# A Hyena mixer's Fourier transforms as plain float32 matmuls, with the convolution in order and wider sums with i

## The chip, the cores and the metric

The kernel runs on one core of one Trainium2 chip. The metric is the device time of one execution in microseconds; the time given for a kernel is the median of several executions.

## The reference: what is computed

One block of a diffusion transformer on a sequence of 1024 positions with 1024 channels, in float32. After a modulated RMS norm, one wide projection gives the inputs of two mixers, differential attention and Hyena; their gated sum goes through an output projection, and a SwiGLU follows. The change touches only the Hyena part:

```python
def hyena_branch(u, ...):                       # u: 1024 positions x 1536 channels
    u = short_conv(u, conv_w, conv_b)           # three taps along the positions
    parts = split(u, 3)                         # 512 channels each
    hk = hyena_filters(...)                     # spectra of 2 filters, made by a small MLP
    z = parts[0]
    for n in range(2):
        z = parts[n + 1] * fftconv(z, hk[:, n], dbias[n])
    return z

def fftconv(u, hk, dbias):                      # a circular convolution of length 2048
    return irfft(rfft(u, n=2048) * hk, n=2048)[:1024] + u * dbias
```

## The kernel before, in words

Channels lie on the 128 partitions, positions along the free axis. The kernel is written for a scheduling layer: the program is recorded in the order of its lines, each instruction with its dependences, and at build time a list scheduler puts the instructions of each engine in order, by the order of recording as the priority and by estimated durations. On the chip every engine works through its own list strictly in that order. So a later part's instruction can stand ahead of an earlier part's where the scheduler saw the engine free; the projections fill TensorE's gaps in this way.

The stages that matter:

1. **Start and filters** (`ORDER`, L26, names the order of recording). `load_mf` (M) loads the transform's matrix; `ada_rows`, `x_stats`, `x_scale` and `modulate` make the normed input `h_hi`, `h_lo`. For four filter blocks (2 filters x 2 groups of 256 channels), `filter_begin`, `filter_mid`, `filter_mid2` and `filter_end` make eight pieces of the filter each (`make`, L378), transform them with TensorE (`spec`, L397, matmuls at L408), combine two results into a sum and a difference (`sd_from_psum`, L255) and finish with butterflies on DVE (`dft8_even`, `dft8_odd`). The spectrum goes to DRAM (`kspec`).
2. **Hyena** (L521 to L671). `raw_tile` (L495) projects one tile of 128 output channels: `wload` loads weights and splits them (`whi` on ACT at L132, `wlo` on DVE), then 2 x 24 matmuls at L140 follow. There are 12 such tiles for Hyena (`praw`) and 16 for the gates (`graw`, recorded behind this stage). `hyena_conv` (L523) loads one `praw` tile into `cv` (one buffer) and applies the three taps: one operation on ACT and two `scalar_tensor_tensor` on DVE (L86 by way of `stt`). It reads every eighth position, so that the result `u` lies ordered by remainder r mod 8. `fftconv` (L541) runs four times: for four pairs of remainders it transposes `u` (L548), copies and splits it (`uh`, `ul`), multiplies by the matrix (L562 to L564, the matrix reloaded and cast each time by `matrix`, L534), and forms sums and differences; then butterflies, the product with the spectrum (`times_k`), butterflies back to `H`, the split `Hh`/`Hl` (L594), and `finish` (L601): inverse matmuls at L614, a copy `yt`, transposes back (L620), and the product into `p`. `hyena_out` writes the result in order, split in two.
3. Behind it come the rest of the gates, attention, the output projection and the SwiGLU, all untouched.

A float32 product is made everywhere from "reduced" operands (type F32R): each operand is split into a high and a low part, and three matmuls hi x hi, lo x hi, hi x lo are summed in PSUM. Plain float32 matmuls occur only in the small sums at L294, L441, L184 and the like; transposes are plain too. `pm_i` (L225) forms a + i b or a - i b for complex numbers stored as 256 real parts followed by 256 imaginary parts. `tt` (L82) records every two-operand operation, so on the profile these all have line L83.

Of the kernel before, what the change touches and what calls it, by code (L numbers as in the profile page):

```python
# [9 lines left out]
F32 = mybir.dt.float32  # L10
# [16 lines left out]
NQUAD, NPAIR, NGEN = 4, 4, 4  # L27
# [4 lines left out]
NMR, NMT = 2, 2  # L32
# [32 lines left out]
def block_kernel(tc, xT, ctxT, cvec, cT, wada1, wada, vecs, lamv, dbias, zT, fw1, fw2, fv, fw3, decay, mfs, mis, rope,  # L65
# [13 lines left out]
    LOENG, M2ENG, HLENG = V, V, V  # L79
# [153 lines left out]
    def dft8_even(S, sign, out):  # L233
        t02, t13 = pair(), pair()
        tt(t02, S[:, 0::2], S[:, 1::2], ALU.add)
        tt(t13, S[:, 0::2], S[:, 1::2], ALU.subtract)
        tt(out[:, 0], t02[:, 0], t02[:, 1], ALU.add)
        tt(out[:, 1], t02[:, 0], t02[:, 1], ALU.subtract)
        pm_i(out[:, 2], t13[:, 0], t13[:, 1], sign)
        pm_i(out[:, 3], t13[:, 0], t13[:, 1], -sign)  # L240

    def dft8_odd(D, sign, out, d3neg=False):
        ab, U, Q = pair(), pair(), pair()
        tt(ab[:, 0], D[:, 2], D[:, 3], ALU.add if d3neg else ALU.subtract)
        tt(ab[:, 1], D[:, 2], D[:, 3], ALU.subtract if d3neg else ALU.add)
        pm_i(U[:, 0], D[:, 0], D[:, 1], sign)
        pm_i(U[:, 1], D[:, 0], D[:, 1], -sign)
        pm_i(Q[:, 0], ab[:, 0], ab[:, 1], sign)
        pm_i(Q[:, 1], ab[:, 0], ab[:, 1], -sign)
# [17 lines left out]
    mft = fl.tile([P, 4, 1024], F32R, name="mft")  # L267
    mfn = fl.tile([P, 8, 2, P], F32R, name="mfn")
# [77 lines left out]

    def load_mf():
        for r in (0, 2, 1, 3):
            raw = wp.tile([P, 1024], F32, tag="wraw", bufs=2, name="mraw")
            nc.sync.dma_start(out=raw, in_=mfs[r])  # L350
            (A.copy if r % 2 == 0 else G.tensor_copy)(out=mft[:, r], in_=raw)
        for j in range(2):
            m5 = mft.rearrange("p a (j h q m) -> p j a h q m", j=2, h=2, q=2)
            ts(mfn[:, 4 * j:4 * j + 4], f(m5[:, j, :, :, 1]), -1.0, None, ALU.mult, ALU.bypass, G)

    def mfm(part, r):

        if part == 2:
            return mfn[:, r, 0], mfn[:, r, 1]
        c0 = r // 4 * 512 + part * P  # L360
        return mft[:, r % 4, c0:c0 + P], mft[:, r % 4, c0 + 256:c0 + 256 + P]
# [3 lines left out]
    def filter_spec(o, c):  # L365
# [12 lines left out]
        def make(r):  # L378
            dec = fg.tile([P, 256], F32, tag="dec", bufs=6, name="dec")
            nc.scalar.dma_start(out=dec, in_=decay[c, :, r])  # L380
            ps = psf()
            cs = slice(r * P, (r + 1) * P)
            for i, (a, b) in enumerate(((hd_hi, fh), (hd_lo, fh), (hd_hi, fo))):
                T.matmul(out=ps, lhsT=a[:, cs], rhs=b, start=i == 0, stop=i == 2)
            x = fp.tile([P, 512], F32, tag="xb", bufs=2, name="gx")
            tt(x.rearrange("p (d c) -> p d c", d=2), ps.rearrange("p (d c) -> p d c", d=2),
               dec.unsqueeze(1).broadcast_to([P, 2, 256]), ALU.mult)
            if r == 0:
                V.memset(x[0:1, 256:512], 0.0)
                tt(x[0:1, 0:256], x[0:1, 0:256], dbt, ALU.add)  # L390
            hi = fg.tile([P, 512], F32R, tag="ghi", bufs=NGEN, name="ghi")
            lo = fg.tile([P, 512], F32R, tag="glo", bufs=NGEN, name="glo")
            A.copy(out=hi, in_=x)
            tt(lo, x, f(hi), ALU.subtract, LOENG)
            gen[r] = (hi, lo)

        def spec(r):  # L397
            rb = (8 - r) % 8
            ps = psf()
            for part, pb in ((0, 0), (1, 2)):  # L400
                out = ps[:, part * 256:(part + 1) * 256]
                ops = []
                for (m, rr, x) in ((part, r, 0), (pb, rb, 1)):
                    mh, ml = mfm(m, rr)
                    xs = slice(x * 256, (x + 1) * 256)
                    ops += [(mh, gen[rr][0][:, xs]), (ml, gen[rr][0][:, xs]), (mh, gen[rr][1][:, xs])]
# [116 lines left out]
    def hyena_conv(m, dst):  # L523
# [5 lines left out]
        v = lambda k: raw[:, k:k + L].rearrange("p (a r) -> p r a", r=8)  # L529
# [4 lines left out]
    def matrix(src):  # L534
        raw = yp.tile([P, 512], F32, tag="mr", bufs=NMR, name="mr")
        nc.sync.dma_start(out=raw, in_=src)
        m = yp.tile([P, 512], F32R, tag="mt", bufs=NMT, name="mt")
        A.copy(out=m, in_=raw)
        return m

    def fftconv(u, o, c, p):  # L541

        S, D_ = quad(), quad()
        for r in (0, 2, 1, 3):
            pt = psf()
            for j, rr in enumerate((r, r + 4)):
                for h in range(2):
                    T.transpose(out=pt[:, j * 256 + h * P:j * 256 + (h + 1) * P], in_=u[:, h, rr], identity=ident)  # L548
            uh = yp.tile([P, 512], F32R, tag="uh", bufs=2, name="uh")
            ul = yp.tile([P, 512], F32R, tag="ul", bufs=2, name="ul")  # L550
            A.copy(out=uh, in_=pt)
            tt(ul, pt, f(uh), ALU.subtract)
            pp = []
            for j in range(2):
                ps = psf()
                xs = slice(j * 256, (j + 1) * 256)
                m = matrix(mfs[r, :, j * 512:(j + 1) * 512])
                for part in range(2):
                    mh = m[:, part * P:(part + 1) * P]
                    ml = m[:, 256 + part * P:256 + (part + 1) * P]  # L560
                    po = ps[:, part * 256:(part + 1) * 256]
                    T.matmul(out=po, lhsT=mh, rhs=uh[:, xs], start=True, stop=False)  # L562
                    T.matmul(out=po, lhsT=ml, rhs=uh[:, xs], start=False, stop=False)
                    T.matmul(out=po, lhsT=mh, rhs=ul[:, xs], start=False, stop=True)  # L564
                pp.append(ps)
            sd_from_psum(pp[0], pp[1], S, D_, SLOT[r])

        def times_k(X, half):
            for b in range(2):
                kk = yp.tile([P, 2, 512], F32, tag="hk", bufs=4, name="kk")  # L570
# [23 lines left out]
        def split(x):  # L594
            hi = yp.tile([P, 2, 512], F32R, tag="hk", bufs=4, name="Hh")
            lo = yp.tile([P, 2, 512], F32R, tag="hk", bufs=4, name="Hl")
            A.copy(out=hi, in_=x)  # L597
            tt(lo, x, f(hi), ALU.subtract, HLENG)
            return [(hi[:, i], lo[:, i]) for i in range(2)]

        def finish(r, Hs):  # L601
            ps = psf()
            for j in range(2):
                hi, lo = Hs[j]
                po = ps[:, j * 256:(j + 1) * 256]
                ops = []
                m = matrix(mis[r, :, j * 512:(j + 1) * 512])
                for part in range(2):
                    mh = m[:, part * P:(part + 1) * P]
                    ml = m[:, 256 + part * P:256 + (part + 1) * P]  # L610
                    cs = slice(part * 256, (part + 1) * 256)
                    ops += [(mh, hi[:, cs]), (ml, hi[:, cs]), (mh, lo[:, cs])]
                for i, (a, b) in enumerate(ops):
                    T.matmul(out=po, lhsT=a, rhs=b, start=i == 0, stop=i == len(ops) - 1)  # L614
# [7 lines left out]
            pv = p[:, :, r:r + 5:4, :]  # L622
# [4 lines left out]
        finish(0, split(H[:, 0:2]))  # L627
        finish(2, split(H[:, 2:4]))
        H = quad()
        dft8_odd(D_, 1, H, d3neg=True)  # L630
        h17, h53 = split(H[:, 0:2]), split(H[:, 2:4])
        finish(1, [h17[0], h53[0]])
        finish(3, [h53[1], h17[1]])

    def hyena_out(c, z):
        for h in range(2):
            uh = z[:, h].rearrange("p r a -> p a r")
            hi = yp.tile([P, L], F32R, tag="hk", bufs=4, name="zhi")
            lo = yp.tile([P, L], F32R, tag="hk", bufs=4, name="zlo")
            A.copy(out=hi.rearrange("p (a r) -> p a r", r=8), in_=uh)  # L640
            tt(lo.rearrange("p (a r) -> p a r", r=8), uh, f(hi).rearrange("p (a r) -> p a r", r=8), ALU.subtract)
# [3 lines left out]
    def part(o, c):  # L645
        p = yp.tile([P, 2, 8, P], F32, tag="u", bufs=3, name="u")
# [857 lines left out]
```

## Time and profile before

| | |
|---|---|
| median of 3 runs | 1945.61 us (1942.84 to 1947.03) |
| profiled execution, its own time | 1944.66 us |
| its span, first to last instruction | 1942.9 us |
| mean granted TensorE clock | 0.943 of full |
| matmul records, DVE instructions, ACT instructions | 8158, 2606, 1306 |
| HBM read, written | 216.93 MB, 75.50 MB |

PE is TensorE's matmul side, PEld its weight loads, DVE VectorE, ACT ScalarE, POOL GpSimd, SP the engine that issues most DMAs. Times are microseconds from the start of the span. In a timeline a row reads: start, length, engine, line, operation, result <- operands, shapes, xcount and, in brackets, how long the engine had been idle before it and which instruction ended that. Rows of one operation that follow each other are merged into one with a count.

### The profile page before, as it was taken

The numbers are of one execution on the slowest core, as the hardware profiler recorded it, in microseconds if no ns is written. First come the engines' busy times: TensorE is split into PE (matmuls) and PEld (weight loads), VectorE is DVE, ScalarE is ACT, GpSimd is POOL, SyncE is SP. The second block draws the span as 40 slices with busy tenths as digits, with TensorE's granted clock in tenths as the row PEclk, the third lists the DMA queues.
The fourth block names the chain that finished last, engine by engine and source line by source line (L and its number), as shares of the span: only waits on it lengthen the run. The fifth ranks groups of instructions, "written<-read, shape, count | busy, mean of one in ns | idle before, by whom it ended". The sixth has DMA issues, their size and how long they took to land.

```text
span 1942.9 us, 23060 instructions
## 1 busy us (share of the span) xinstructions
PE 1738.5 (89%) x8158; PEld 1395.7 (72%) x8158; DVE 1466.7 (75%) x2606; ACT 847.5 (44%) x1306; POOL 72.3 (4%) x72
## 2 busy tenths in 40 slices
PE   7999859567789999999999997889999999798996
PEld 3588647456678888888787775668888888586874
DVE  5898798886946348989885868787776657868667
ACT  4533425334242237666675634453333334444421
POOL 1000000000000121112000000000000000000001
PEclk9899969697989999999999998989999999898998
DMA  9244615234366374443725674322325222434384
GB/s 337 69 171 153 214 58 195 98 129 151 115 251 211 115 218 122 129 135 109 236 90 193 219 241 159 134 85 99 112 104 167 92 76 76 147 104 152 128 302 154
DMA packets 130659, 293.95 MB, mean 151 GB/s; under 512 B 14659, under 2 KB 35919, under 8 KB 129264
## 3 DMA queue, kind: packets, MB, share of 16 engines
q1 hardware_dynamic: 124320, 284.82, 43.1%
q10 hardware_dynamic: 6224, 7.66, 1.3%
q8 instruction: 64, 1.05, 0.2%
q14 instruction: 51, 0.42, 0.1%
HBM read 216.93 MB, written 75.50 MB: 151 GB/s over the span
## 4 chain that ended last, share of the span: by engine, by line
PE 62%; DVE 21%; DMA 8%; ACT 3%; issue 3%; SPq 1%; DVEq 0%; ACTq 0%
PE pj L1151 24%; PE ps L140 22%; DVE pair L83 4%; PE S L840 3%; DVE quad L83 3%; PE psf L408 2%; DVE u L86 2%; PE pt L862 2%; PE psf L614 1%; DMA mr<-mfs 1%; DVE wlo L83 1%; DMA dacc_t<-dacc 1%; PE pv L871 1%; DMA cv<-praw 1%; PE pv L873 1%
## 5 line engine op out<-in xcount | busy, mean ns | idle before, releaser
L83 DVE TENSOR_TENSOR wlo<-wraw,whi 128x512 fp32r<-128x512 f32 (+2 forms) x199 | 167.4, 850 | 94.0 <-ACT whi L132 72.7
L140 PE MATMUL ps<-h_hi,wlo 128*128 128x512 f32 x640 | 179.7, 408 | 3.0 <-DVE wlo L83 3.0
L1151 PE MATMUL pj<-hfc,whi 128*128 128x512 f32 x720 | 178.7, 390 | 0.0
L140 PE MATMUL ps<-h_hi,whi 128*128 128x512 f32 x640 | 171.9, 399 | 3.1 <-ACT h_hi L453 1.9
L140 PE MATMUL ps<-h_lo,whi 128*128 128x512 f32 x640 | 171.4, 394 | 0.0
L1151 PEld LDWEIGHTS pj<-hfc,whi 128*128 128x128 f32 x720 | 135.3, 188 | 28.7
L140 PEld LDWEIGHTS ps<-h_hi,wlo 128*128 128x128 f32 x640 | 121.8, 195 | 27.6 <-DVE wlo L83 4.5
L140 PEld LDWEIGHTS ps<-h_hi,whi 128*128 128x128 f32 x640 | 119.5, 191 | 28.0 <-ACT h_hi L453 3.8
L1151 PE MATMUL pj<-hfb,whi 128*128 128x512 f32 x480 | 127.5, 410 | 11.8 <-ACT whi L1143 11.8
L140 PEld LDWEIGHTS ps<-h_lo,whi 128*128 128x128 f32 x640 | 118.9, 190 | 22.9
L1151 PE MATMUL pj<-hfa,whi 128*128 128x512 f32 x480 | 121.6, 396 | 3.3 <-ACT whi L1143 3.3
L1143 ACT CAST whi<-wraw 128x512 fp32r<-128x512 f32 x120 | 72.4, 621 | 114.3 <-PE pj L1151 84.8
L1151 PEld LDWEIGHTS pj<-hfb,whi 128*128 128x128 f32 x480 | 94.0, 197 | 36.1 <-ACT whi L1143 13.4
L1143 ACT CAST whi<-s 128x512 fp32r<-128x512 f32 x90 | 54.5, 620 | 139.9 <-DVE s L83 89.8
L132 ACT CAST whi<-wraw 128x1024 fp32r<-128x1024 f32 (+2 forms) x94 | 88.2, 940 | 55.3 <-PE ps L140 33.8
L840 PE MATMUL S<-KS,Q 128*128 128x512 f32 (+1 forms) x384 | 107.6, 374 | 2.8 <-DVE pr L844 2.4
L1151 PEld LDWEIGHTS pj<-hfa,whi 128*128 128x128 f32 x480 | 90.8, 190 | 25.2 <-ACT whi L1143 4.4
L1151 PE MATMUL pj<-hfc,wlo 128*128 128x512 f32 x360 | 97.1, 392 | 5.3 <-DVE wlo L83 5.3
L614 PE MATMUL psf<-Hh,mt 128*128 128x256 f32 x128 | 37.2, 389 | 71.8 <-ACT Hh L597 71.8
L501 ACT COPY gt<-ps 128x512 f32<-128x512 f32 x56 | 32.7, 587 | 132.4 <-PE ps L140 88.1
L614 PEld LDWEIGHTS psf<-Hh,mt 128*128 128x128 f32 x128 | 29.3, 280 | 75.5 <-ACT Hh L597 75.2
L1151 PEld LDWEIGHTS pj<-hfc,wlo 128*128 128x128 f32 x360 | 67.3, 188 | 20.9 <-DVE wlo L83 7.0
(486 smaller groups left out, 3803.2 us busy)
## 6 DMA issues: line engine op xcount, KB each, us to landing
wraw<-win SPq DMA_DIRECT2D x46, 512.0 KB, 3.6
wada_t<-wada SPq DMA_DIRECT2D x32, 512.0 KB, 5.4
wraw<-wgate SPq DMA_DIRECT2D x28, 512.0 KB, 3.2
wraw<-wupf SPq DMA_DIRECT2D x28, 512.0 KB, 3.7
araw<-ad SPq DMA_DIRECT2D x44, 256.0 KB, 4.2
w_ada<-wada SPq DMA_DIRECT2D x16, 512.0 KB, 6.3
kspec<-quad SPq DMA_DIRECT2D x8, 1024.0 KB, 3.9
mr<-mfs SPq DMA_DIRECT2D x32, 256.0 KB, 3.7
```

The costliest lines, as they stand in the source:

```text
L83: (eng or V).tensor_tensor(out=out, in0=a, in1=b, op=op)
L86: V.scalar_tensor_tensor(out=out, in0=a, scalar=s, in1=b, op0=op0, op1=op1)
L132: A.copy(out=hi, in_=raw)
L140: T.matmul(out=ps, lhsT=w[:, k * P:(k + 1) * P], rhs=xs[k][j], start=start and i == 0, stop=stop and i == len(seq) - 1)
L408: T.matmul(out=out, lhsT=a, rhs=b, start=i == 0, stop=i == len(ops) - 1)
L501: A.copy(out=gt, in_=ps)
L614: T.matmul(out=po, lhsT=a, rhs=b, start=i == 0, stop=i == len(ops) - 1)
L840: T.matmul(out=S[:, :cn], lhsT=Q[j][:, i, qt * P:(qt + 1) * P], rhs=KS[i][:, c0:c0 + cn], start=j == 0, stop=j == 1)
L862: T.transpose(out=pt[:, b * 256 + qt * P:b * 256 + (qt + 1) * P], in_=av[qt][:, kt * P:(kt + 1) * P], identity=ident)
L871: T.matmul(out=pv[:, :256], lhsT=VH[:, kt], rhs=ah[:, xs], start=kt == 0, stop=False)
L1143: A.copy(out=hi, in_=src)
L1151: T.matmul(out=ps, lhsT=w[a][:, k * P:(k + 1) * P], rhs=xs[k][b], start=i == 0, stop=i == 11)
```

## The change

- Transform matmuls (filter, forward, inverse) take plain float32 operands: one call in place of three. The splits that fed them (`ghi`/`glo`, `uh`/`ul`, `Hh`/`Hl`) go.
- The matrices come from DRAM as two halves, hi and lo; they are now summed once (on DVE, four operations of 128x1024 each) and stay on chip: the forward one `mf` from the start on, in the pool that lives through Hyena, with its negated imaginary part `mfn` made by ACT; the inverse one `mi` at the opening of the Hyena pool, loaded through the `hk` buffers. The reload and cast in every transform (`matrix`) goes.
- `hyena_conv` keeps the order of positions; the transposes and the product in `finish` step by eight instead, and `hyena_out` reads and writes in order.
- `pm_i` forms both a + i b and a - i b in two operations of 512 elements, one operand with its halves swapped, in place of four of 256.
- Buffers: eight pieces of a filter (`gx`, a buffer of its own), `hk` three instead of four, `ut` two.

```diff
-NQUAD, NPAIR, NGEN = 4, 4, 4
+NQUAD, NPAIR, NGEN = 4, 4, 8
-NMR, NMT = 2, 2
+NHK, NUT = 3, 2
     def pm_i(out, a, b, sign):
-        o1, o2 = (ALU.subtract, ALU.add) if sign > 0 else (ALU.add, ALU.subtract)
-        tt(out[:, RE], a[:, RE], b[:, IM], o1)
-        tt(out[:, IM], a[:, IM], b[:, RE], o2)
+        minus, plus = (ALU.subtract, ALU.add) if sign > 0 else (ALU.add, ALU.subtract)
+        o = out.rearrange("p s (q c) -> p (s q) c", q=2)
+        a2, b2 = [v.rearrange("p (q c) -> p q c", q=2) for v in (a, b)]
+        tt(o[:, 0::3], a2, b2[:, ::-1], minus)
+        tt(o[:, 1:3], a2[:, ::-1], b2, plus)
...
-        pm_i(U[:, 0], D[:, 0], D[:, 1], sign)
-        pm_i(U[:, 1], D[:, 0], D[:, 1], -sign)
+        pm_i(U, D[:, 0], D[:, 1], sign)
...
+    def matrices(dst, src, tile):
+        d5 = dst.rearrange("p (j r) q m -> p j r (q m)", j=2)
+        for r in (0, 2, 1, 3):
+            raw = tile()
+            nc.sync.dma_start(out=raw, in_=src[r])
+            r4 = raw.rearrange("p (j h x) -> p j h x", j=2, h=2)
+            tt(d5[:, :, r], r4[:, :, 0], r4[:, :, 1], ALU.add)
...
-            hi = fg.tile([P, 512], F32R, tag="ghi", bufs=NGEN, name="ghi")
-            lo = fg.tile([P, 512], F32R, tag="glo", bufs=NGEN, name="glo")
-            A.copy(out=hi, in_=x)
-            tt(lo, x, f(hi), ALU.subtract, LOENG)
-            gen[r] = (hi, lo)
+            gen[r] = x
...
-                for i, (a, b) in enumerate(ops):
-                    T.matmul(out=out, lhsT=a, rhs=b, start=i == 0, stop=i == len(ops) - 1)
+                T.matmul(out=out, lhsT=mfm(part, r), rhs=gen[r][:, 0:256], start=True, stop=False)
+                T.matmul(out=out, lhsT=mfm(pb, rb), rhs=gen[rb][:, 256:512], start=False, stop=True)
...
-        v = lambda k: raw[:, k:k + L].rearrange("p (a r) -> p r a", r=8)
+        v = lambda k: raw[:, k:k + L]
...
+    mi = yp.tile([P, 8, 2, P], F32, name="mi")
+    matrices(mi, mis, lambda: yp.tile([P, 1024], F32, tag="hk", bufs=NHK, name="mraw"))
...
-            A.copy(out=uh, in_=pt)
-            tt(ul, pt, f(uh), ALU.subtract)
+            A.copy(out=ut, in_=pt)
...
-                m = matrix(mfs[r, :, j * 512:(j + 1) * 512])
...
-                    T.matmul(out=po, lhsT=mh, rhs=uh[:, xs], start=True, stop=False)
-                    T.matmul(out=po, lhsT=ml, rhs=uh[:, xs], start=False, stop=False)
-                    T.matmul(out=po, lhsT=mh, rhs=ul[:, xs], start=False, stop=True)
+                    T.matmul(out=ps[:, part * 256:(part + 1) * 256], lhsT=mf[:, r + 4 * j, part],
+                             rhs=ut[:, j * 256:(j + 1) * 256], start=True, stop=True)
...
-            A.copy(out=hi, in_=x)
-            tt(lo, x, f(hi), ALU.subtract, HLENG)
-            return [(hi[:, i], lo[:, i]) for i in range(2)]
...
+                    T.matmul(out=ps[:, j * 256:(j + 1) * 256], lhsT=mi[:, r + 4 * j, part],
+                             rhs=Hs[j][:, part * 256:(part + 1) * 256], start=part == 0, stop=part == 1)
...
-            pv = p[:, :, r:r + 5:4, :]
+            pv = by_r(p)[:, :, r:r + 5:4, :]
```

## Rows read from the trace of the kernel before

**Rows 1.** The page, part 1: busy us (share) xinstructions

```profile
PE 1738.5 (89%) x8158; PEld 1395.7 (72%) x8158; DVE 1466.7 (75%) x2606; ACT 847.5 (44%) x1306; POOL 72.3 (4%) x72
```

**Rows 2.** Windows: length, busy us of PE, PEld, DVE, ACT, POOL; PEclk, DMA, GB/s

```profile
100.00:184.00 84.00, 84.00 (x481) 73.53 (x480) 72.15 (x123) 27.22 (x44) 0.00 (x0) 1.00 0.42 152
184.00:558.00 374.00, 271.25 (x1277) 221.17 (x1276) 310.18 (x390) 150.27 (x195) 1.54 (x24) 0.84 0.42 142
258.00:292.00 34.00, 13.54 (x47) 11.05 (x48) 32.23 (x40) 10.34 (x12) 0.13 (x2) 0.51 0.20 65
...
600.00:700.00 100.00, 100.00 (x517) 85.25 (x516) 39.62 (x65) 25.58 (x42) 5.15 (x4) 1.00 0.44 145
```

**Rows 3.** Who PE waits for, 184 to 558: us in total, times, longest us

```profile
PE psf L614 <- ACT Hh L597: 71.8, 9, 19.1
PE psf L562 <- ACT mt L538: 8.5, 9, 1.7
...
PE psf L564 <- DVE ul L83: 3.4, 6, 0.8
PE ps L140 <- DVE wlo L83: 3.0, 5, 1.1
...
PE psf L548 <- DVE u L86: 1.5, 1, 1.5
```

**Rows 4.** Timeline of PE, first transform, 250 to 320

```profile
251.01 3.79 PE L140 MATMUL ps<-h_hi,whi 128*128 128x512 f32 x16
272.91 0.80 PE L614 MATMUL psf<-Hh,mt 128*128 128x256 f32 x2 [18.11 <-ACT Hh L597]
274.31 0.58 PE L614 MATMUL psf<-Hl,mt 128*128 128x256 f32 x1 [0.61 <-DVE Hl L83]
274.69 0.64 PE L614 MATMUL psf<-Hh,mt 128*128 128x256 f32 x2
...
285.95 0.80 PE L614 MATMUL psf<-Hh,mt 128*128 128x256 f32 x2 [2.99 <-ACT Hh L597]
```

**Rows 5.** Timeline of DVE, butterflies of the first transform; last row: the fourth

```profile
225.02 1.26 DVE L83 TENSOR_TENSOR wlo<-wraw,whi 128x1024 fp32r<-128x1024 f32 x1
...
244.92 1.29 DVE L83 TENSOR_TENSOR quad<-pair 128x512 f32<-128x512 f32 x2
...
251.01 1.43 DVE L83 TENSOR_TENSOR pair<-pair 128x256 f32<-128x256 f32 x4
252.35 2.19 DVE L86 SCALAR_TENSOR_TENSOR u<-cv,vec,u 128x1024 f32<-128x1024 f32 x1
...
285.87 1.22 DVE L83 TENSOR_TENSOR wlo<-wraw,whi 128x1024 fp32r<-128x1024 f32 x1
...
508.43 1.22 DVE L83 TENSOR_TENSOR wlo<-wraw,whi 128x1024 fp32r<-128x1024 f32 x1
```

**Rows 6.** Chain of waits (start, us, what), 0 to 600; then two of PE's timeline

```profile
59.99 6.10 PE ada_ps L294 x14
66.09 1.91 PE bc L441 x4
...
114.74 4.78 PE psf L408 x40
...
297.18 0.60 PE L548 MATMUL psf<-ident,u 128*128 128x128 f32 x4
...
594.35 0.70 PE L184 MATMUL bc<-dg,ones 128*128 128x256 f32 x2 [0.54 <-DVE dg L89]
```

**Rows 7.** Groups of DVE and ACT, 184 to 558: busy us, mean ns | idle before

```profile
L86 DVE SCALAR_TENSOR_TENSOR u<-cv,vec,u 128x1024 f32<-128x1024 f32 x24 | 52.4, 2184 | 14.1 <-ACT u L92 8.5 <-issue 5.2
...
L86 DVE SCALAR_TENSOR_TENSOR quad<-pair 128x1024 f32<-128x1024 f32 x18 | 21.2, 1220 | 0.0
...
L83 DVE TENSOR_TENSOR u<-u,psf 128x512 f32<-128x512 f32 x16 | 11.0, 688 | 16.7 <-PE psf L620 16.7
...
L597 ACT CAST Hh<-quad 128x1024 fp32r<-128x1024 f32 x16 | 16.7, 1043 | 77.5 <-DVE quad L83 67.2 <-DVE quad L86 10.1
```

More of the change, by code (lines that the diff above doesn't have):

```diff
@@ L78, in block_kernel @@
     AE = (V,)
-    LOENG, M2ENG, HLENG = V, V, V
+    M2ENG = V
     RENG, RLENG = V, G
@@ L238, in dft8_even @@
         tt(out[:, 1], t02[:, 0], t02[:, 1], ALU.subtract)
-        pm_i(out[:, 2], t13[:, 0], t13[:, 1], sign)
-        pm_i(out[:, 3], t13[:, 0], t13[:, 1], -sign)
+        pm_i(out[:, 2:4], t13[:, 0], t13[:, 1], sign)
     def dft8_odd(D, sign, out, d3neg=False):
@@ L245, in dft8_odd @@
         tt(ab[:, 1], D[:, 2], D[:, 3], ALU.subtract if d3neg else ALU.add)
[L246 to L249 removed]
+        pm_i(U, D[:, 0], D[:, 1], sign)
+        pm_i(Q, ab[:, 0], ab[:, 1], sign)
         fl_ = lambda t: t.rearrange("p a b -> p (a b)")
@@ L266, in block_kernel @@
     fl = fstk.enter_context(pool("filt", side="right"))
-    mft = fl.tile([P, 4, 1024], F32R, name="mft")
-    mfn = fl.tile([P, 8, 2, P], F32R, name="mfn")
+    mf = fp.tile([P, 8, 2, P], F32, name="mf")
+    mfn = fl.tile([P, 8, P], F32, name="mfn")
     hd_hi = fl.tile([65, L], F32R, name="hd_hi")
@@ L345, in load_x @@
             nc.sync.dma_start(out=xk[k], in_=xT[k])
-    def load_mf():
[L348 to L354, printed above, removed]
+    def matrices(dst, src, tile):
[5 more added lines that the diff above has]
+            tt(d5[:, :, r], r4[:, :, 0], r4[:, :, 1], ALU.add)
+    def load_mf():
+        matrices(mf, mfs, lambda: wp.tile([P, 1024], F32, tag="wraw", bufs=2, name="mraw"))
+        act(mfn, mf[:, :, 1], AF.Copy, scale=-1.0)
     def mfm(part, r):
[L358 to L361, printed above, removed]
+        return mfn[:, r] if part == 2 else mf[:, r, part]
     fg = fstk.enter_context(pool("fgen", side="right"))
@@ L384, in make @@
                 T.matmul(out=ps, lhsT=a[:, cs], rhs=b, start=i == 0, stop=i == 2)
-            x = fp.tile([P, 512], F32, tag="xb", bufs=2, name="gx")
+            x = fg.tile([P, 512], F32, tag="gx", bufs=NGEN, name="gx")
             tt(x.rearrange("p (d c) -> p d c", d=2), ps.rearrange("p (d c) -> p d c", d=2),
@@ L532, in hyena_conv @@
         stt(dst, v(2), w[2], dst, ALU.mult, ALU.add)
[L534 to L539, printed above, removed]
+    mi = yp.tile([P, 8, 2, P], F32, name="mi")
+    matrices(mi, mis, lambda: yp.tile([P, 1024], F32, tag="hk", bufs=NHK, name="mraw"))
     def fftconv(u, o, c, p):
+        by_r = lambda t: t.rearrange("p h (a r) -> p h r a", r=8)
         S, D_ = quad(), quad()
@@ L547, in fftconv @@
                 for h in range(2):
-                    T.transpose(out=pt[:, j * 256 + h * P:j * 256 + (h + 1) * P], in_=u[:, h, rr], identity=ident)
-            uh = yp.tile([P, 512], F32R, tag="uh", bufs=2, name="uh")
-            ul = yp.tile([P, 512], F32R, tag="ul", bufs=2, name="ul")
-            A.copy(out=uh, in_=pt)
-            tt(ul, pt, f(uh), ALU.subtract)
+                    T.transpose(out=pt[:, j * 256 + h * P:j * 256 + (h + 1) * P], in_=by_r(u)[:, h, rr], identity=ident)
+            ut = yp.tile([P, 512], F32, tag="ut", bufs=NUT, name="ut")
+            A.copy(out=ut, in_=pt)
             pp = []
@@ L569, in times_k @@
             for b in range(2):
-                kk = yp.tile([P, 2, 512], F32, tag="hk", bufs=4, name="kk")
+                kk = yp.tile([P, 2, 512], F32, tag="hk", bufs=NHK, name="kk")
                 nc.sync.dma_start(out=kk, in_=kspec[o][c][:, half * 4 + b * 2:half * 4 + b * 2 + 2])
@@ L603, in finish @@
             for j in range(2):
[L604 to L607, printed above, removed]
                 for part in range(2):
[L609 to L614, printed above, removed]
+                    T.matmul(out=ps[:, j * 256:(j + 1) * 256], lhsT=mi[:, r + 4 * j, part],
+                             rhs=Hs[j][:, part * 256:(part + 1) * 256], start=part == 0, stop=part == 1)
             yt = fp.tile([P, 512], F32, tag="xb", bufs=2, name="yt")
@@ L626, in fftconv @@
         dft8_even(S, 1, H)
-        finish(0, split(H[:, 0:2]))
-        finish(2, split(H[:, 2:4]))
+        finish(0, [H[:, 0], H[:, 1]])
+        finish(2, [H[:, 2], H[:, 3]])
         H = quad()
         dft8_odd(D_, 1, H, d3neg=True)
-        h17, h53 = split(H[:, 0:2]), split(H[:, 2:4])
-        finish(1, [h17[0], h53[0]])
-        finish(3, [h53[1], h17[1]])
+        finish(1, [H[:, 0], H[:, 2]])
+        finish(3, [H[:, 3], H[:, 1]])
     def hyena_out(c, z):
         for h in range(2):
[L637 to L641, printed above, removed]
+            hi = yp.tile([P, L], F32R, tag="hk", bufs=NHK, name="zhi")
+            lo = yp.tile([P, L], F32R, tag="hk", bufs=NHK, name="zlo")
+            A.copy(out=hi, in_=z[:, h])
+            tt(lo, z[:, h], f(hi), ALU.subtract)
             rawdma(zs[0][c * 2 + h], hi)
@@ L645, in part @@
     def part(o, c):
-        p = yp.tile([P, 2, 8, P], F32, tag="u", bufs=3, name="u")
+        p = yp.tile([P, 2, L], F32, tag="u", bufs=3, name="u")
         for h in range(2):
```

12 lines of the change are left out of this document (removed).

## The prediction

> **What bounds the kernel now.** I read the page first: PE is busy 89% of the span, DVE 75%, ACT 44% [rows 1]. That is a mean, so the second view is the table of windows [rows 2]. The edits lie in two stages. In the filter stage (100 to 184 us here) PE is busy 84.00 of 84 us. In the Hyena stage (184 to 558) it is busy 271 of 374 while DVE has 310, and behind it (600 to 700) PE is again full. So the Hyena stage is the only one with PE time to win, and one rule follows that I use throughout: work that PE does as filler (the projections of L140) and does not get done by 558 is done later in a full stage. **A shorter Hyena stage is not by itself a shorter kernel; the end moves by what PE's work grows minus what PE's idle time shrinks.**
>
> The third view, who PE waits for in that stage, names the idle time [rows 3]: 71.8 us for the cast `Hh` at L597, 8.5 for the cast `mt`, 3.4 for `ul`, 3.0 for `wlo`, 1.5 for `u`. The timeline of PE shows the shape of one transform [rows 4]: projections stop at 254.8, PE stands 18.11 us, starts L614 at 272.91, and loses the clock meanwhile (0.51 of full, that is mostly 1.2 GHz, over 258 to 292 [rows 2]). The same picture stands in the second and third transform (the longest wait is 19.1 us [rows 3]); in the fourth it is shorter: 71.8 less 2 x 18.1, 19.1 and the three short ones of 2.99 leaves some 7.5. The timeline of DVE says why [rows 5]: from the last sums of the forward transform until H, DVE works on the butterflies without a gap. Two prepared pairs of weights are all that PE has to chew on; the next `wlo` comes at 285.87, the last was at 225.02. In the one place where the butterflies leave a slot, the first transform has a convolution step (252.35, 2.19 us); the fourth has a `wlo` (508.43), which is one more raw tile for PE and explains its short wait.
>
> **The change part by part.**
>
> *Plain float32 matmuls.* By the code, 384 + 192 + 192 = 768 matmuls of 256 columns (L408, L562 to 564, L614) become 256 calls. Forty of them stand 4.78 us on the chain, 0.1195 each [rows 6]: 91.8 us. A plain call shows up as two records: the two calls of L441 are four on the chain; and 14 records of plain matmuls at L294 take 6.10 us, 0.436 per record of 512 columns [rows 6]. By columns I estimate 0.218 for 256, so 0.436 a call, 111.6 us in all: **+19.8 us of PE work.** Bounds: the only records of 256 plain columns in the trace, two in L184, last 0.70 together [rows 6], at most 0.35 each, which would give 179 us (+87); the low end is a call as cheap as the three that it replaces (0). I take the long run of L294, because the L184 pair starts from a standing engine and its 0.70 holds one full latency. In the filter stage no gap takes this up, but the filler moves behind it, which costs the same.
> The Trainium skill (FP8 and Floating Point Precision, TensorE Precision Notes) says that true FP32 takes four passes through the array. By that rule a call is four passes against three, one third more work; rows 6 agree (0.436 against 3 x 0.1195), and it is the rule that speaks against this change.
>
> *Splits gone* (`ghi`/`glo`, `uh`/`ul`, `Hh`/`Hl`, 64 casts `mt` with 64 loads of 256 KB). In the filter stage this frees ACT and DVE, but PE has no gap to give: nothing. In the Hyena stage: PE starts on H itself, without the cast of 1.04 us [rows 7], and without the stop for `Hl` (272.91 to 274.31 where two matmuls elsewhere need 0.43: 0.97 us) [rows 4]. The waits for `mt` and `ul` go: 8.5 + 3.4. What is late next is the copy `ut`, which stands where `uh` stood.
>
> *Sums with i.* Four narrow operations take 1.43 us [rows 5], two wide ones 1.29 (the row at 244.92): 0.14 each time, four times between the spectrum and H, 0.6 us. A reversed operand is not in the trace: 0 to doubling (plus 1.29); I take 0, since only blocks of 256 are swapped and each is read straight.
>
> *Convolution in order.* Its two DVE steps read every eighth element and take 2184 ns each, 24 of them; the same operation on 1024 contiguous elements takes 1220 [rows 7]. So 23 us of DVE go in the stage, but on PE's wait only the one step in the slot, 0.97 us in three of four transforms, and the 1.5 us that PE waits for `u`. With DVE lighter I also let the 3.0 for `wlo` go.
> The stride moves on: 64 transposes of `u` and 16 products with `p` now step by eight. Transposes: four take 0.60 us [rows 6], 0.15 each; between no change and doubling, 0 to +9.6. I take +3, since a part of them runs where PE waits anyway. Products: 688 ns [rows 7], between that and 1.8 times (the ratio of 2184 to 1220), 0 to +8.8; two of four per transform stand before the odd half of H, I take +2.
> The Trainium skill (SBUF — State Buffer, the note on cachelines of 16 bytes) says that a step over more than four fp32 elements pays at each access. The convolution rows agree; by that rule both moved strides pay in full, the upper bounds above.
>
> *Loads of the matrices.* Four sums of 1024 elements on DVE (1.22 each, 4.9 us) for the forward matrix at the start and four for the inverse one at the stage's opening; 64 reloads on SP's queue go. The first lie beside the chain of PE work on L294 [rows 6], the second beside projections that are prepared. Both 0, or +4.9 each if the cover is gone, for the loads stand in front of the first `cv` on SP.
>
> **Sum.** Long waits: 0.6 + 0.97 + 1.04 + 0.97 = 3.6, three times, and 2.6 in the fourth: -13.4. The wait of 2.99 at 285.95 [rows 4], three times: the cast of 1.04 goes, and PE comes later from its longer even half, so all of it, -9.0. `mt`, `ul`, `u`, `wlo`: -16.4. Together -38.8; against it +19.8 + 3 + 2. **-14 us.** The profiled execution took 1944.66 us (span 1942.9), 0.95 below the median of 1945.61. Forecast: **1931 us.** The measurement can tell about 0.2% (4 us) from no change.
>
> **Rivals.**
> 1. *More filler in the slot.* If the faster convolution is through before the butterflies, the slot at 252 goes to a `wlo` in the first three transforms too, as in the fourth [rows 5]. One raw tile is 48 matmuls of L140; 16 of them take 3.79 us [rows 4], 11 us in all. Three times: -33 more, 1898 us. For it: the step to be saved is the one in the slot. Against: `cv` has one buffer, so a step may be pending all the same.
> 2. *Less filler, slower.* The stretches between the butterflies get shorter (six convolution steps per transform lose 0.96 us each, 5.8), and if only one pair of weights instead of two is ready when the butterflies begin, PE stands 11 us longer each time. It decides from two transforms on: -14 + 22 = +8, 1953 us; three give 1964. For it: the order is fixed at build time by estimated durations, and the engine waits in order. Against: DVE and ACT have more air to prepare a pair.
> 3. *The strides pay in full*, all on PE's path: +9.6 + 8.8 instead of 5, which leaves -0.6: 1944 us, no difference. For it the 2184 ns; against it, half of these operations lie off the path. The cacheline rule above is the same mechanism.
> 4. *The edit does not reach the instruction*: if plain matmuls ran as single records, the work term would turn to a gain and 55.8 us of records (256 x 0.218) stood for 91.8: -36 in place of +19.8, 1875 us. L294 and L441, plain by the code, show pairs, so I give this hardly anything.
>
> **How the numbers follow.** Forecast as worked out: 0.50 (its own range 1918 to 1939). Rival 1: 0.20. Rival 2: 0.17. Rival 3: 0.10, of which most lies within 0.2%. Rival 4: 0.03. Faster by over 0.2%: 0.50 + 0.20 + 0.03, and 0.01 of rival 3: 0.74. Same (within 0.2%): 0.09, the rest of rival 3. Slower: 0.17. The range takes in rival 1 whole (1898, with 3 us for the work term) and rival 2 up to two transforms: 1895 to 1952.
>
> **What would show it.** Right: records of L408's successor at about 0.21 to 0.22 us distance; four waits of PE before the inverse matmuls of 14 to 16 us (the last some 5); the second wait of 2.99 gone; convolution steps near 1.2 us; fewer rows of `graw` work done when the Hyena stage ends, although it ends tens of us earlier (the convolution steps alone give DVE 23). Wrong: waits before the inverse matmuls under 10 us (rival 1) or over 20 (rival 2); products with `p` at 1.25 us and transposes 0.3 apart (rival 3); or a stage behind Hyena in which PE is not full, for then the filler that was put off costs nothing and all of that would be won.

## The result, and the profile after

| | before | after |
|---|---|---|
| median, 4 runs each, side by side | 1944.22 us (1936.91 to 1947.03) | **1893.64 us** (1890.29 to 1900.03) |
| profiled execution, its span | 1944.66, 1942.9 us | 1900.03, 1898.2 us |
| mean granted TensorE clock | 0.943 | 0.960 |
| HBM read | 216.93 MB | 202.25 MB |

The ratio is 0.9748, with the interval 0.9716 to 0.9781: 50.6 us faster. The forecast was 14 us faster (1931), its range began at 1895, and the median lies 1.4 us below that. The profiled execution of the kernel after is the slowest of its four, so its trace shows 44.7 of the 50.6 us.

The page's part 1 answers to [rows 1]. PE has fewer records and is busier, DVE and ACT lost 68 and 91 us of work.

```profile
PE 1743.5 (92%) x7902; PEld 1388.9 (73%) x7902; DVE 1398.8 (74%) x2478; ACT 756.5 (40%) x1193; POOL 64.5 (3%) x68
```

The table of windows answers to [rows 2] (length, then busy us of PE, PEld, DVE, ACT and POOL, granted clock, DMA share, GB/s). The three stretches are the filter stage, the Hyena stage, and one behind it.

```profile
100.00:168.00 68.00, 68.00 (x306) 57.26 (x305) 52.45 (x78) 10.76 (x17) 0.00 (x0) 1.00 0.39 139
168.00:478.00 310.00, 259.56 (x1123) 207.22 (x1122) 261.94 (x309) 80.02 (x114) 1.59 (x24) 0.92 0.37 127
525.00:620.00 95.00, 95.00 (x432) 79.12 (x431) 26.83 (x41) 19.01 (x27) 5.15 (x4) 1.00 0.32 111
```

The Hyena stage ends at 478 instead of 559 us, 81 us earlier, and PE stands 50 us in it instead of 103. Before and behind it PE is as full as it was. The kernel gains less than 81 because projections were put off: 996 matmuls of L140 had run by the end of the stage before, 876 after. The 120 that are missing cost 0.229 us each, the spacing at which they follow each other (16 in 3.79 us [rows 4], which holds the last one's latency), so 27.5 us come later.

Who PE waits for in the Hyena stage answers to [rows 3] (us in total, times, longest). L578 holds the inverse matmuls (L614 before), L543 the forward ones, L536 and L585 the transposes. The 71.8 us for `Hh` are now 33.5 us for the butterflies' own result, `mt` and `ul` are gone, and `u` stands at 1.8.

```profile
PE psf L578 <- DVE quad L83: 33.5, 4, 19.2
PE psf L585 <- ACT yt L581: 7.6, 11, 0.7
PE ps L140 <- DVE wlo L83: 2.9, 3, 1.2
PE psf L536 <- issue: 2.0, 1, 2.0
PE psf L536 <- DVE u L86: 1.8, 1, 1.8
PE psf L543 <- ACT ut L538: 1.4, 1, 1.4
```

The four waits in front of the inverse matmuls are not alike. The timeline of PE (start, length, engine, line, operation, and in brackets the idle time and what ended it) shows the first transform in its first two rows and the third in the last two:

```profile
237.37 3.79 PE L140 MATMUL ps<-h_hi,whi 128*128 128x512 f32 x16
245.49 3.78 PE L578 MATMUL psf<-quad,mi 128*128 128x256 f32 x8 [4.34 <-DVE quad L83]
...
365.56 3.79 PE L140 MATMUL ps<-h_hi,whi 128*128 128x512 f32 x16
388.50 3.78 PE L578 MATMUL psf<-quad,mi 128*128 128x256 f32 x8 [19.15 <-DVE quad L83]
```

18.11 us became 4.34 in the first transform [rows 4], and nothing changed in the third. The timeline of DVE says why, with the butterflies of the first transform (first three rows) and of the third:

```profile
226.38 1.28 DVE L83 TENSOR_TENSOR pair<-pair 128x512 f32<-128x512 f32 x2
227.59 1.22 DVE L83 TENSOR_TENSOR wlo<-wraw,whi 128x1024 fp32r<-128x1024 f32 x1
228.72 2.35 DVE L86 SCALAR_TENSOR_TENSOR quad<-pair 128x1024 f32<-128x1024 f32 x2
...
369.33 1.28 DVE L83 TENSOR_TENSOR pair<-pair 128x512 f32<-128x512 f32 x2
370.53 1.28 DVE L86 SCALAR_TENSOR_TENSOR u<-cv,vec,u 128x1024 f32<-128x1024 f32 x1
371.73 2.35 DVE L86 SCALAR_TENSOR_TENSOR quad<-pair 128x1024 f32<-128x1024 f32 x2
```

This is the slot of [rows 5]. Before, its contents in the four transforms were u, u, u, `wlo`; after, `wlo`, `wlo`, u, `wlo`.

**Where PE's time went.** From the starts of all matmuls I give each record the distance at which its like follow at full clock (a record of 256 columns 0.120 in the split form and 0.215 in the plain one, a transpose 0.108) and call that work; a distance more than 0.5 us longer is a gap, and what remains is the rest, more than half of it in stretches of half clock.

| us | work | gaps | of them long waits in the Hyena stage | rest |
|---|---|---|---|---|
| before | 1629.0 | 203.8 | 18.3 + 18.3 + 19.2 + 7.3 = 63.1 | 93.2 |
| after | 1647.0 | 152.2 | 4.5 + 4.7 + 19.3 + 5.6 = 34.1 | 82.4 |

+18.0 - 51.6 - 10.8 is -44.4, the 44.7 us of the span. The three add up to the span by the way they are made; what they show is where the time went.

### The profile page after: what moved, and what is told of

It reads as the page before. It is cut to its first block, busy times and chain, and to the rows that moved or that the text cites. A ratio compares the mean times of both kernels' runs of the same rounds, so it can differ in the third digit from the quotient of the medians.

```text
span 1898.2 us, 22173 instructions
## 1 busy us (share of the span) xinstructions
PE 1743.5 (92%) x7902; PEld 1388.9 (73%) x7902; DVE 1398.8 (74%) x2478; ACT 756.5 (40%) x1193; POOL 64.5 (3%) x68
## 3 DMA queue, kind: packets, MB, share of 16 engines
HBM read 202.25 MB, written 75.50 MB: 146 GB/s over the span
## 4 chain that ended last, share of the span: by engine, by line
PE 61%; DVE 21%; DMA 10%; issue 4%; ACT 2%; SPq 0%; DVEq 0%; ACTq 0%
PE pj L1114 25%; PE ps L140 19%; DVE pair L83 4%; PE S L803 3%; DVE quad L83 3%; DVE wlo L83 2%; DMA wada_t<-wada 2%; PE pt L825 2%; PE psf L398 2%; PE psf L399 2%; PE psf L578 1%; PE psf L543 1%; DMA wraw<-wdown 1%; DMA dacc_t<-dacc 1%; PE pv L834 1%
## 5 line engine op out<-in xcount | busy, mean ns | idle before, releaser
L140 PE MATMUL ps<-h_hi,wlo 128*128 128x512 f32 x640 | 173.8, 400 | 2.9 <-DVE wlo L83 2.9
L140 PE MATMUL ps<-h_lo,whi 128*128 128x512 f32 x640 | 169.4, 396 | 0.0
L140 PE MATMUL ps<-h_hi,whi 128*128 128x512 f32 x640 | 167.6, 396 | 1.3 <-ACT gt L492 1.3
L140 PEld LDWEIGHTS ps<-h_hi,wlo 128*128 128x128 f32 x640 | 119.1, 190 | 27.5 <-DVE wlo L83 4.3
L140 PEld LDWEIGHTS ps<-h_hi,whi 128*128 128x128 f32 x640 | 119.4, 189 | 26.0 <-ACT gt L492 1.7
L140 PEld LDWEIGHTS ps<-h_lo,whi 128*128 128x128 f32 x640 | 119.6, 189 | 23.9
L1114 PEld LDWEIGHTS pj<-hfb,whi 128*128 128x128 f32 x480 | 93.8, 196 | 36.1 <-ACT whi L1106 13.4
L83 DVE TENSOR_TENSOR wlo<-s,whi 128x512 fp32r<-128x512 f32 x90 | 60.2, 686 | 26.1 <-PE pj L1114 26.1
L1114 PE MATMUL pj<-hfb,wlo 128*128 128x512 f32 x240 | 69.2, 412 | 8.5 <-DVE wlo L83 8.5
```

What stands on the lines that cost most here:

```text
L83: (eng or V).tensor_tensor(out=out, in0=a, in1=b, op=op)
L140: T.matmul(out=ps, lhsT=w[:, k * P:(k + 1) * P], rhs=xs[k][j], start=start and i == 0, stop=stop and i == len(seq) - 1)
L1114: T.matmul(out=ps, lhsT=w[a][:, k * P:(k + 1) * P], rhs=xs[k][b], start=i == 0, stop=i == 11)
```

## The experiments

The ratios below are to the kernel before on the same chip, with their intervals.

**The parts one by one.** *plain_only* is the kernel before with plain matmuls and resident matrices; the convolution and the sums stay as they were.

```diff
-                    T.matmul(out=po, lhsT=mh, rhs=uh[:, xs], start=True, stop=False)
-                    T.matmul(out=po, lhsT=ml, rhs=uh[:, xs], start=False, stop=False)
-                    T.matmul(out=po, lhsT=mh, rhs=ul[:, xs], start=False, stop=True)
+                    T.matmul(out=ps[:, part * 256:(part + 1) * 256], lhsT=mf[:, r + 4 * j, part], ...
...
```

> Plain matmuls, matrices kept on chip and no splits, but the convolution by remainders and four narrow sums as before. Theory slot: in DVE's order a weight split wlo now stands in the butterflies' slot of the first and second transform, so their two long waits of PE fall from 18 to some 5 us; with the gone waits for mt, ul, Hl and the second Hh (25 us) and a shorter half clock, against 18 us more PE work, this alone gives most of the gain: 30 to 45 us below before (1900 to 1915). Theory parts as priced in the prediction (slot plays no role): -38.8 without 0.97 x 3, 0.6 x 4 and 1.5, so -32, against +19.8: 12 us below, 1932. Theory length (the gain follows the DVE time taken out of the Hyena stage, of which the convolution is nearly half): about half of the gain, 25 us.

*conv_only* is the kernel before with the convolution in order, and the stride moved to the transposes and the product:

```diff
-        v = lambda k: raw[:, k:k + L].rearrange("p (a r) -> p r a", r=8)
+        v = lambda k: raw[:, k:k + L]
...
+                    T.transpose(..., in_=by_r(u)[:, h, rr], identity=ident)
...
+            pv = by_r(p)[:, :, r:r + 5:4, :]
```

> Before, with the convolution in order alone (transposes, products and hyena_out follow it). In the slots stands u in the first three transforms, as before. Theory slot: the convolution gives PE little: 1 us of each of three long waits and 1.5 for u, against dearer products: 0 to 6 us below before (1938 to 1944). Theory parts: the same, -4.4 + 5, no change. Theory length: 23 us of DVE less, so 15 to 25 us below before.

*sums_only* is the kernel before with the new `pm_i`.

> Before, with the sums with i as two wide operations alone. Slots as before. Theories slot and parts: 0.6 to 0.9 us of each long wait, 2 to 4 us below before. Theory length: 27 pairs in the Hyena stage at 0.2 us, 5 us below.

Measured: 1922.17 (0.9896, 0.9868 to 0.9924), 1923.13 (0.9896, 0.9857 to 0.9935) and 1941.57 us (0.9997, 0.9981 to 1.0014), beside 1943.28: 21 us, 20 us, and nothing that stands clear of the noise. The three add up to some 42 of the 50.6 us; the intervals are too wide to say whether the parts gain more together than apart. With plain_only the slots turned to `wlo`, `wlo`, u, `wlo`; with conv_only they stayed u, u, u, `wlo`. So the convolution gained 20 us without the slot, and neither the slot nor the sum of my terms explains that. The theory of the slot missed twice here (30 to 45 us for plain_only, 0 to 6 for conv_only). Both gains lie nearest to the theory of length, which missed in sums_only (5 us). The next run tells the two apart: it adds no DVE time, so by length it would stay within 5 us of the kernel after.

**The slot.** *after_slots_undone* records the raw tiles that fill it later, and nothing else:

```diff
-    raws(2, 3, 6, 7)
+    raws(2, 3)
     u1 = part(0, 1)
+    raws(6, 7)
...
-    raws(8, 9, 10, 11)
+    raws(8, 9)
...
     fftconv(p00, 1, 0, p10)
+    raws(10, 11)
```

> The changed kernel with two raw tiles recorded later (6, 7 behind part(0, 1); 10, 11 behind the third transform), so that a convolution step stands in the slot of the first three transforms, as in the kernel before; the instructions are the same, only their order differs. Theory slot: the first two long waits of PE go back from 4.5 to 14 to 16 us and the half clock with them; 20 to 30 us above after (1914 to 1924). Theory parts and theory length: no instruction is added, within 5 us of after (1889 to 1899).

Measured: 1914.61 us (0.985, 0.9823 to 0.9877), 21 more than the kernel after, so the theory of length fails. Its timelines of DVE and PE in the first transform:

```profile
228.34 1.27 DVE L86 SCALAR_TENSOR_TENSOR u<-cv,vec,u 128x1024 f32<-128x1024 f32 x1
```

```profile
246.30 3.78 PE L578 MATMUL psf<-quad,mi 128*128 128x256 f32 x8 [15.36 <-DVE quad L83]
```

The convolution step is back in the slot, and the wait is 15.36 us for 4.34. The number of projections that PE has between the last forward matmul and the first inverse one shows what the slot is worth. In the four transforms it is 95, 88, 94 and 126 before; 135, 134, 75 and 124 after; and 87, 86, 76 and 120 with the slots undone. That is 48 fewer in each of the first two, exactly one raw tile.

*plain_slots_undone* makes the same edit in plain_only.

> plain_only with the raw tiles 6, 7 and 10, 11 recorded later, as in after_slots_undone, so that a convolution step stands in the first three slots. Theory slot: the two long waits come back and with them 18 to 24 us: 1940 to 1947, so the plain matmuls without the slots are worth nothing. Theory that the gone splits and reloads carry the gain of plain_only: within 6 us of it (1916 to 1928).

Measured: 1938.77 us (0.9968, 0.9946 to 0.999), a little under the expected band and, by the two ratios, 14 us above plain_only. Without the slots the plain matmuls are worth about 6 us (2 to 10): what they save in gaps and in the rest (8 and 14 us in the trace) they nearly spend in work (18).

*after_third_slot* records four gate tiles ahead of the last convolution, so that a pair is ready for the third slot:

```diff
     hyena_out(0, p10)
+    for j in range(4):
+        raw_tile(24 + j, graw[j])
     p11 = part(2, 1)
...
-    for j in range(NGT):
+    for j in range(4, NGT):
```

> The changed kernel with four gate tiles recorded ahead of part(2, 1), so that wlo stands in the slot of all four transforms. Theory slot: the third long wait falls from 19.2 to some 5 us and the half clock around it from 24 to 7 us; 12 to 20 us below after (1874 to 1882). Theories parts and length: the same work, within 5 us of after.

Measured: **1876.70 us** (0.9666, 0.9642 to 0.9691), 17 below the kernel after and the best of all. The third slot on DVE, the wait behind it on PE, and the waits of the stage:

```profile
368.98 1.22 DVE L83 TENSOR_TENSOR wlo<-wraw,whi 128x1024 fp32r<-128x1024 f32 x1
```

```profile
386.88 2.81 PE L578 MATMUL psf<-quad,mi 128*128 128x256 f32 x8 [3.88 <-DVE quad L83]
```

```profile
PE psf L578 <- DVE quad L83: 15.1, 4, 4.6
```

The control, *after_two_gates*, moves two gate tiles instead of four; that leaves the convolution step in the third slot.

> Control for after_third_slot: only two gate tiles recorded ahead of part(2, 1), which leaves a convolution step in the third slot. Theory slot: the third long wait stays near 19 us, within 5 us of after (1888 to 1900). If it was the earlier gate tiles and not the slot that gained 17 us there: 6 to 12 us below after.

Measured: 1893.34 us (0.9718, 0.9697 to 0.974), the time of the kernel after, with its third wait:

```profile
386.74 3.78 PE L578 MATMUL psf<-quad,mi 128*128 128x256 f32 x8 [19.16 <-DVE quad L83]
```

So it is not the moved tiles as such: the slot decides. By the ratios this kernel is 6 us faster than the kernel after, but their intervals overlap; that of after_third_slot lies below both. *before_third_slot* is the edit of after_third_slot in the kernel before.

> The kernel before with the same four gate tiles recorded ahead of part(2, 1): u, u, wlo, wlo in the four slots. Theory slot: the third long wait falls from 19.1 to some 8 us, 8 to 18 us below before (1926 to 1936). Other theories: no change.

Measured: 1934.19 us (0.9965, 0.9951 to 0.998), 7 us faster, just short of the expected band. Who PE waits for, against [rows 3]:

```profile
PE psf L614 <- ACT Hh L597: 58.0, 9, 18.1
PE psf L562 <- ACT mt L538: 9.4, 8, 2.9
...
PE psf L614 <- DVE Hl L83: 4.8, 5, 2.4
```

The third wait fell from 19.2 to 5.5 us, but the waits for `mt` and `Hl`, which the change abolishes, grew (8.5 to 9.4, 2.4 to 4.8). The lever works without the change, and gains less.

**Does the end follow PE's work?** *after_double_forward* issues each forward matmul twice (64 more calls, 128 records; each result is overwritten by the same):

```diff
+                    for _ in range(2):
                         T.matmul(out=ps[:, part * 256:(part + 1) * 256], lhsT=mf[:, r + 4 * j, part], ...
```

> The changed kernel with each forward transform matmul (L543) issued twice, the second over the first: 64 calls, 128 records more, 27.5 us of PE work at 0.215 a record, all in the Hyena stage; slots as in after. Theory conservation (the end moves by PE work less PE idle time): 20 to 30 us above after (1914 to 1924), a little being taken up by idle time in front of the sums. If instead the Hyena stage is bound by DVE and the filler behind it has room: under 10 us above.

Measured: 1918.40 us (0.9883, 0.9854 to 0.9912), 25 more than the kernel after, for 27.6 us of added work, although the stage has idle time:

```profile
PE psf L579 <- DVE quad L83: 24.1, 4, 13.3
```

The longest wait shrank from 19.2 to 13.3 us and still most of the added work reached the end. The two profiled executions lie closer together, 13.8 us (here the fastest of four, there the slowest): +27.6 of work, -7.5 of gaps, -7.1 of rest. So the idle time of the stage takes up a part of added work, but does not swallow it: this is the test of the forecast's rule, and it held.

**Why the convolution alone gains.** Two kernels lengthen one link of it in conv_only: *conv_act_twice* issues the operation on ACT twice, *conv_dve_twice* the two on DVE.

```diff
-        act(dst, v(1), AF.Identity, ...)
+        for _ in range(2):
+            act(dst, v(1), AF.Identity, ...)
```

> conv_only with the convolution's ACT operation issued twice (the second writes the same values again), so that ACT has its old 2.4 us back and DVE does not. Theory A (conv_only gains because ACT's step no longer stands in front of the casts uh and mt that PE waits for): back to within 8 us of before (1935 to 1946). Theory D (it gains because DVE's two steps are shorter): stays within 6 us of conv_only (1917 to 1929).

```diff
-        stt(dst, v(0), w[0], dst, ALU.mult, ALU.add)
-        stt(dst, v(2), w[2], dst, ALU.mult, ALU.add)
+        for k in (0, 0, 2, 2):
+            stt(dst, v(k), w[k], dst, ALU.mult, ALU.add)
```

> conv_only with each of the two DVE steps of the convolution issued twice (the outer taps count twice, so the result is another convolution), 5.1 us of DVE per half in place of 2.6, where before had 4.4. Theory D: back to before or a little above (1940 to 1955). Theory A: within 6 us of conv_only (1917 to 1929).

Measured: 1938.63 (0.9972, 0.9954 to 0.9991) and 1946.01 us (0.9994, 0.9975 to 1.0013), beside 1944.42 for the kernel before. Each took back most or all of the 20 us, so neither of the two theories holds alone: a longer ACT step costs, and so do longer DVE steps. The wait rows of conv_only, conv_act_twice and conv_dve_twice, in this order, show where:

```profile
PE psf L615 <- ACT Hh L598: 66.2, 8, 17.2
...
PE psf L563 <- ACT mt L538: 4.6, 6, 1.8
...
PE psf L563 <- ACT uh L552: 1.3, 2, 0.7
```

```profile
PE psf L616 <- ACT Hh L599: 80.3, 7, 25.9
```

```profile
PE psf L615 <- ACT Hh L598: 86.0, 7, 24.7
```

A convolution is one chain: load `cv`, one step on ACT (2361 ns before, 1246 in conv_only and in the kernel after), two on DVE, then the only `cv` buffer comes free for the next. In conv_only the gaps (reckoned as above) in front of the forward matmuls shrink from 13.1 to 6.0 us for `mt` and `uh` and from 4.3 to 0 for `ul`, those in front of the transposes of `u` from 3.9 to 0.6, and the long waits from 63.0 to 56.4: 21 us in all, about the gain. The two longer kernels do not lose it by the same way back. Their small gaps stay short (5.7 and 3.0 us in all), and it is the long waits that grow, to 70.8 and 76.6 us: in the third transform PE has 53 and 56 projections in front of the wait where conv_only has 94, most of one raw tile less. So the runs show that the length of this chain counts on either engine. How a shorter chain gained its 20 us is read from the waits and not shown by an experiment of its own, and that the one buffer ties the links together was not tried.

**One miss.** *after_wlo_on_pool* moves the weights' split of the Hyena stage from DVE to POOL, so that the slot needs no DVE.

```diff
+    LO[0] = G
     u0 = part(0, 0)
...
+    LO[0] = V
```

> The changed kernel with the split wlo of the raw tiles and gates on POOL from the Hyena stage to its end. Theory slot: what PE lacks in the butterflies is a prepared pair of weights, and DVE is what cannot prepare it; on POOL the pair comes whenever ACT has cast its half, so all four long waits fall under 5 us; 10 to 25 us below after (1869 to 1884), unless POOL, with a second reader beside DVE, takes several us a split or slows DVE: then the waits for wlo grow in their place and the time rises.

Measured: 1898.22 us (0.9769, 0.9739 to 0.9799), no gain. The group on POOL:

```profile
L83 POOL TENSOR_TENSOR wlo<-wraw,whi 128x1024 fp32r<-128x1024 f32 x8 | 48.2, 6029 | 35.6 <-ACT whi L132 35.6
```

A split takes 6.03 us there for 1.22 on DVE, and the gate tiles, the third transform's filler, are recorded after the switch back. The third wait stayed at 19.1 and the second grew to 12.1 us. It decides nothing about the slot.

## Why the prediction was wrong in size

The sign held, and so did the rule behind it: the end moves by PE's work minus PE's idle time (after_double_forward tests it). The size did not: the likeliest case had given 14 us, and 50.6 came. The step that failed is the choice that **the slot goes on holding a convolution step in the first three transforms**. In the first two it holds a `wlo`. Undoing that alone costs 21 us, about the 11 each that rival 1 had priced. Rival 1 gave 1898 and had a chance of 0.20; it came close in time, but partly by luck. Its sum was another: three slots, not two, and less from the other terms. Its reason was wrong as well: it expected the faster convolution to clear the slot, but conv_only has that convolution and keeps u there, and plain_only, with the old convolution, has `wlo`.

What the other terms gave shows in after_slots_undone, which has the slots as forecast. It is 29 us faster than before, not 14.

| us | forecast | after_slots_undone, trace |
|---|---|---|
| PE's work | +19.8 | +18.0 |
| long waits | -13.4 | -9.8 |
| the other waits | -9.0 - 16.4 = -25.4 | -26.7 |
| strides of transposes and products | +5 | none on the path |
| half clock and rest | not priced | -10.6 |
| sum | -14 | -29.1 |

So of the 36.6 us between forecast and measurement about 21 belong to the slot, and 15 to the terms of this table: the rest that had no price (10.6), the strides (5), and 3 in work and the other waits, less the 3.6 that the long waits fell short (the third, with 76 projections before it where there were 94, fell by 1.2 us only). Within the other waits I also let two go that stayed: `wlo` (3.0, now 2.9) and `u` (1.5, now 1.8).

- **Work: right.** Eight records on the chain take 1.80 us, 0.225, and 1.79, 0.224; the spacing of the run gives 0.215, for 0.218 estimated. A call is two records, 0.43 us, against 0.36 for three split ones. The rule of four passes (the Trainium skill, FP8 and Floating Point Precision, TensorE Precision Notes) has the direction right, but counted as the prediction did, four passes against three, it gives a third more where the trace has a fifth. The prediction's own numbers, 0.436 against 3 x 0.1195, were a fifth too; to say that they agree with a third was a misreading.
- **Transposes: wrong.** I took +3 and bounded at +9.6. My 0.15 for one was a quarter of a row that holds the last one's latency. Four transposes of the strided `u` take 0.44 us on the chain, and the distance of one to the next is 0.108 in both kernels. The stride does cost something, but in the weight load: `u` is the operand that is loaded. The rule on cachelines (the Trainium skill, SBUF — State Buffer, the note on cachelines of 16 bytes) shows there, 189 ns a load for 140 (the medians are 192 in conv_only, which has the stride, and 141 in plain_only, which has not). A load lasts longer than the 0.108 us from one transpose to the next, so loads and matmuls overlap. The chain of waits after (start, us, what), then the groups of weight loads in the Hyena stage before and after (busy us, mean ns, idle before):

```profile
201.14 1.80 PE psf L543 x8
202.94 0.44 PE psf L536 x4
203.37 0.94 PE ps L140 x4
204.31 1.79 PE psf L543 x8
```

```profile
L548 PEld LDWEIGHTS psf<-ident,u 128*128 128x128 f32 x64 | 7.5, 140 | 4.4 <-issue 2.5 <-DVE u L86 1.9
```

```profile
L536 PEld LDWEIGHTS psf<-ident,u 128*128 128x128 f32 x64 | 9.5, 189 | 5.5 <-issue 2.6 <-DVE u L86 2.2
```

- **Products and convolution steps: sizes right, worth wrong.** The product went from 688 to 1116 ns, inside the bounds, and the cacheline rule shows here too; but PE's waits name no product. The convolution steps went to 1280 ns. The groups of DVE in the Hyena stage answer to [rows 7] (busy us, mean ns, idle before):

```profile
L86 DVE SCALAR_TENSOR_TENSOR u<-cv,vec,u 128x1024 f32<-128x1024 f32 x24 | 30.7, 1280 | 12.6 <-ACT u L92 11.4 <-issue 0.4
...
L83 DVE TENSOR_TENSOR u<-u,psf 128x512 f32<-128x512 f32 x16 | 17.9, 1116 | 6.9 <-PE psf L585 6.8
L83 DVE TENSOR_TENSOR pair<-pair 128x512 f32<-128x512 f32 x18 | 11.6, 682 | 0.0
...
L83 DVE TENSOR_TENSOR mi<-mraw 128x512 f32<-128x512 f32 x4 | 2.6, 680 | 0.0
```

I let the convolution count only where it stood in front of a long wait, and with the stride it came out near zero. Alone it gained 20 us, in the trace through the small waits and, for a third, the long ones.
- **Sums with i: not contradicted**, 0.6 us a transform forecast and nothing clear of the noise found (sums_only: up to 4 us faster, up to 3 slower); a reversed operand costs nothing (682 ns for 512 elements, as for the plain [rows 5] sums: two in 1.29). **Sums of the matrices: right in worth, too high in size**: each adds 512 elements, not the 1024 that the section on the change gives too, and takes 680 ns for the 1.22 us I took.
- **Half clock: left out.** I quoted 0.51 for the stretch around the first wait and put no price on it. From the clock record, half clock lasts 34.1, 34.1, 34.1 and 17.1 us in the four transforms before; with the slots undone 17.1, 17.1, 23.9 and 13.6, and 10.2, 6.8, 23.9 and 3.4 after. But the rest does not follow that: it fell by 10.6 us with the slots undone and by 10.8 after, so in these traces the two slots gained in gaps alone. By the same reckoning it fell by 13 in plain_only and 14 in plain_slots_undone, and by 0.5 in conv_only and 1.7 in before_third_slot, where half clock became shorter too (222 us of the whole span before, 198 and 205 there). So most of this term came with the plain matmuls; by which way was not taken apart.
- **Rivals 2 to 4: not seen.** No pair was lost, the strides did not pay in full, and plain calls are two records each.
- **The range** was to take in rival 2 up to two transforms, which the prediction puts at 1953; its end at 1952 misses that by 1 us and decides nothing here.

**Why the slot holds a `wlo` only after** is shown as far as the order goes: with the same recorded order, plain_only turns it, and after_slots_undone turns it back by the order of recording. That a pair was not ready on the chip before is not the reason. Casts and splits pair off in order: before, the cast `whi` that belongs to the `wlo` of 285.87 is the one at 241.73, done almost 10 us before the slot opens at 252.35, and still the convolution step stands there. With the slots undone it is the same, a cast at 216.95 and the step at 228.34; after, the cast at 216.21 is followed by its `wlo` at 227.59. ACT's timelines, before, with the slots undone, and after:

```profile
241.73 1.05 ACT L132 CAST whi<-wraw 128x1024 fp32r<-128x1024 f32 x1
```

```profile
216.95 1.05 ACT L132 CAST whi<-wraw 128x1024 fp32r<-128x1024 f32 x1
```

```profile
216.21 1.05 ACT L132 CAST whi<-wraw 128x1024 fp32r<-128x1024 f32 x1
```

What stands in the slot is thus a choice of the list made at build time. Which of the gone instructions or freed buffers made the scheduler choose otherwise stays open.

## What to carry to other kernels

Where one engine's list has a single gap in a long serial stretch, ask which instruction the scheduler will put there after the change: one slot was worth 7 to 17 us here, where the forecast was 14 for the whole change. That the operands are ready on the chip does not say that the list has their instruction there: read the order. Check the end by work plus idle time of the engine that is full elsewhere, not by the length of the stage: the stage became 81 us shorter, the kernel 50. The order of recording is a lever of its own: four tiles recorded earlier took a further 17 us.

## What was not expected of the hardware

- The transposes of an operand with a step of eight fp32 follow each other at the same 0.108 us as contiguous ones, although each weight load takes 189 for 140 ns; a DVE product with that step, read and written, takes 1116 for 688 ns.
- After waits of the same length (19.2 and 19.15 us, third transform) the clock came back at different times. Before, PE resumed at 443.4, and the granted clock was half for 20 us more; after, it resumed at 388.5, and it was half for 9.5. The windows show it, before and then after; PE was busier in the latter (8.31 of 10 us for 7.68 and 6.61). That this made the difference was not tried.

```profile
443.00:453.00 10.00, 7.68 (x32) 6.80 (x32) 9.29 (x16) 4.80 (x8) 0.00 (x0) 0.50 0.22 77
453.00:463.00 10.00, 6.61 (x22) 5.09 (x22) 7.61 (x8) 3.81 (x5) 0.00 (x0) 0.50 0.33 108
463.00:473.00 10.00, 8.82 (x57) 7.21 (x55) 5.14 (x5) 7.29 (x9) 0.00 (x0) 0.99 0.50 186
```

```profile
388.00:398.00 10.00, 8.31 (x20) 5.80 (x20) 9.21 (x13) 1.06 (x2) 0.00 (x0) 0.50 0.00 0
398.00:408.00 10.00, 9.10 (x48) 7.54 (x49) 7.34 (x7) 3.49 (x6) 0.00 (x0) 1.00 0.32 105
```

- POOL takes 6.03 us for an elementwise subtraction of 128x1024 that DVE does in 1.22.
